# The hot gates' comparisons ahead of the weights, pieces on GpSimd, and a reordered mixer in a dense two-block kernel

## The chip, the cores and the metric

The kernel runs on one core of a Trainium2 chip. The metric is the device time of one execution in microseconds (us), lower is better. Engines are named as in the profile: PE multiplies matrices, DVE and ACT work on vectors, POOL is GpSimd, SP issues transfers. In the code they are `P`, `V`, `A`, `G` and `nc.sync`. Each engine has one queue and works through it in order; work of one engine waits for another's by semaphores.

## The reference

256 tokens of width 1024 go through two blocks, all in 32-bit floats. The first block has two layers: differential attention and a gated short convolution, each followed by a SwiGLU FFN with layer norms (LN). The second block has one layer of three parts, each added to its input behind an RMS norm:

```python
x = x + parallel_mixer(rms_norm_2(x, mix_norm_g), ...)              # mLSTM heads and stick-breaking heads
x = x + memory_cross_attention(rms_norm_2(x, xattn_norm_g), rms_norm_2(mem, mem_norm_g), ...)
x = x + peer_ffn(rms_norm_2(x, ffn_norm_g), ...)
return rms_norm_2(x, final_norm_g)
```

In the mixer, q and k of the four mLSTM heads pass a causal depthwise convolution of four taps (`qk_m = silu(causal_depthwise_conv(qk_m, conv_w, conv_b))`). The mLSTM part and the stick-breaking part are each normalised by head (`head_rms_norm`) and, side by side, multiplied by `w_out`. The memory is 256 further tokens; its keys and values are `rms_norm_2(mem) @ wkv`. PEER picks, for each token and each of 8 heads, the best 16 of 128 x 128 = 16384 experts and adds `gate * gelu(u_e . x) * v_e` over them.

## The kernel before

**Weights.** Every product of 32-bit floats is made of three matmuls (`mm3`, L328 to L331): both factors are split into a high part and a low part, `h` and `l`, and h·h, h·l and l·h are summed in PSUM. The weights come in chunks of 1 MB in the order of a plan. The class `Stream` (`W`, L195 to L262) brings them: SP issues the transfer into one of two `raw` tiles (L215); each chunk has two halves of 1024 columns, k = 0 and 1; `pre` has ACT copy a half to its high part `wh` (L231); `split` has the engine named in `W.sub[k]` subtract it from raw to give the low part `wl` (L243). `V` and `G` in `W.sub` are DVE and POOL. `W.look` says by how many halves the split runs ahead of the half that PE is about to use. The next raw transfer is issued when both halves of a chunk are split, as it reuses the tile.

**Boundaries.** Between stages the result of the last matmuls gets the residual added, is normalised and transposed to be the next stage's `xT`. The 256 tokens are two tiles t = 0 and 1 of 128. `finish_any` and, with `two=True`, `finish_two` write the order: `last_mm` (the last matmuls), `fa` (`ln_a` L412/L413 or `add_a` L458/L463, on DVE), `fb` (`ln_b` L418 to L428; `rms_b` L443 to L453, with the power (x+eps)^-0.5 on POOL, L320), `to_T` (PE transposes L370, ACT L373, DVE L378). Splits of the next weights stand between these steps, on DVE or POOL. There are three LN boundaries of the first block (`early=0`; about 134 to 150, 322 to 346 and 427 to 445 us), the one from the last FFN to the mixer (`two=True`, a LN and the RMS norm, about 612 to 650), mixer to cross attention (`early=2`, 784 to 815) and cross attention to PEER (`early=1`, 865 to 882). Matmuls on the memory (`mem_v`, `mem_k0`, `mem_k1`), which depend on nothing in the boundary, are put into it as filler; its chunks are named mv0 to mv3 here.

**The memory's copy.** The normalised memory `mT` lies in a pool that ends with the last FFN. Behind the boundary two POOL transfers (L965) copy it to a new tile, and the freed space is reused by the mixer's tiles, `vs` (L1002) among them.

**The mixer.** `mqk` (L1046 to L1064) makes q and k of one head: matmuls, a copy into a padded tile, the first tap (`tensor_scalar`, L1059, on DVE), then three more taps (L1062, on DVE); it does this for two parts, so eight taps a head. `W.sub = [G, V]` gives every k = 0 half here to POOL. A loop over `hs` then interleaves the mLSTM's outputs with the stick-breaking heads (`sb_z`, `sb_c`, `sb_v`). `ml_norm` (L1126) scales the mLSTM half of `mixed`, `sb_norm` (L1187 to L1198) the other half: a gain product on POOL (L1192) and a product by 1/rms on DVE (L1198). The products with `w_out` are interleaved with these; L362 makes a low part of a transposed operand.

**PEER's u-stage.** All 16384 experts are computed densely, in 64 chunks of two halves. The gates of the last 33 steps of this loop, the hot stage, are made from the selected slots beside the loop: for a group g of tokens `hot_make(g)` compares indices with a table on DVE (one product L1571 gives `oi`, four L1574 give `oj`, in one of two halves of the tiles OI and OJ); `hot_mm(g)` does four matmuls of 32-bit floats, eight in the trace (L1581), then multiplies `big` by the result on DVE (L1584) and copies the rest on ACT (L1585). One step e of the loop is in program order:

```python
w(k)                      # split of a later half: ACT L231, then DVE L243
while pend: pend.pop(0)() # gelu of the chunk before, on ACT
proj_stat(...)            # 24 matmuls on PE
hot_make(e - 1)           # DVE
gated()                   # the gelu's product by its gates, DVE or POOL
hot_mm(e - 2, 2 * c)      # PE, DVE L1584, ACT L1585
gated()
```

Of the kernel before, what the change touches and what calls it, by code (L numbers as in the profile page):

```python
# [197 lines left out]
class Stream:  # L198
# [36 lines left out]
    def split(self, n):  # L235
        while self.ns < min(n, 2 * len(self.plan)):
# [5 lines left out]
            for s in self.parts(self.ns):  # L242
                self.sub[k].tensor_tensor(l[:, s], self.R[i][:, k * HW:(k + 1) * HW][:, s], h.bitcast(F32)[:, s],  # L243
                                             op=OP.subtract)
# [19 lines left out]
def body(ctx, tc, I, O):  # L264
# [210 lines left out]
    def finish_two(acc, items, fa, fb, x, fa0, fb0):  # L475
# [3 lines left out]
        W.split(2 * W.i + 3)  # L479
        W.sub = [G, G]  # L480
# [24 lines left out]
    def finish_any(acc, items, fa, fb, x, fa0=(), fb0=(), two=False, early=0, first=2, warm=0):  # L505
# [14 lines left out]
        if early:  # L520
            last_mm(acc, items, 1, 1)
            W.split(2 * W.i + first + early)
# [3 lines left out]
        fa(1, 1)  # L526
        if callable(src0):
            src0 = src0()
# [431 lines left out]

    finish(acc, items, lambda t, nb: ln_a(t, nb, acc, h3), ln_rms, xT, [lambda: mem_v(0)], [lambda: mem_v(1)], True, early=0)
    f2ctx.close()
    mTo, mT = mT, new_xT()
    for k in range(2):
        G.dma_start(mT[k], mTo[k])  # L965
# [79 lines left out]
    def mqk(h, k):  # L1045
# [11 lines left out]
        for a in range(2):  # L1057
            ft = a * 4 + h
            V.tensor_scalar(y[:, a, :], pad[:, a, 0:256], cols[:, 24 + 4 * ft:25 + 4 * ft], cols[:, 56 + ft:57 + ft],  # L1059
                            op0=OP.mult, op1=OP.add)  # L1060
# [65 lines left out]
    def ml_norm(ss):  # L1126
        rs = inv_sqrt(ss, 8, "rs8")
        for t in (1, 0):
            for h in range(4):
                hs = slice(h * 128, h * 128 + 128)  # L1130
                V.tensor_scalar(mixed[:, t, hs], mixed[:, t, hs], rs[:, 4 * t + h:4 * t + h + 1], None, op0=OP.mult)
# [55 lines left out]
    def sb_norm():  # L1187
        ss = sm([128, 16], name="ss16", bufs=1)
        for t in range(2):
            sq = wp.tile([128, D], F32, name="r")[:, 0:512]  # L1190
            A.activation(sq, mixed[:, t, 512:], AF.Square)
            G.tensor_tensor(mixed[:, t, 512:], mixed[:, t, 512:], gmx[:, 512:], op=OP.mult)  # L1192
# [17 lines left out]
    W.sub = [G, V]  # L1210
# [18 lines left out]
    for hs in range(8):  # L1229
        if hs > 0:  # L1230
            sq_proj(hs // 2, hs % 2)
        if hs == 6:
            ml_norm(ss8)
# [4 lines left out]
        if i >= 0:  # L1238
            if k == 0:
                sb_z(i)  # L1240
            elif i < 2:
# [12 lines left out]
    sb_c(4)  # L1254
    to_T_half(mixed[:, 0, :], 0, mxT, 0)
    sb_c(5)
# [12 lines left out]
    W.sub = [G, V]  # L1269
    sb_norm()  # L1270
    mem_v(2)
    W.sub = [V, V]
    for t in range(2):
        to_T_half(mixed[:, t, :], t, mxT, 1)
    items = o_items(mxT, "wout", 2)
# [328 lines left out]
    for c in range(NC):  # L1604
# [4 lines left out]
        for k in range(2):  # L1609
            w(k)  # L1610
# [10 lines left out]
            e = 2 * c + k - HOT0  # L1621
# [4 lines left out]
            if 1 <= e < 34:  # L1626
                if e < 33:
                    hot_make(e - 1)
                gated()
                if e > 1:  # L1630
                    hot_mm(e - 2, 2 * c)
            gated()
        pend.append(lambda c=c, ps=ps: gelu(c, ps))
# [79 lines left out]
```

## Time and profile before

| what | us |
|---|---|
| median of three runs | 1720.41 |
| lowest and highest run | 1719.59, 1721.41 |
| the profiled execution | 1723.32 |
| its span in the trace | 1721.5 |
| mean granted PE clock in it | 0.992 |

The profiled execution is 2.9 us over the median, and 1.8 us of it lie outside the span. How to read the rows of the profile: a row of the timeline has the start, the duration, the engine, the line of the kernel, the operation, `output<-input`, partitions x elements, and `xN` where N instructions follow each other without a gap; `[3.03 <-DVE big L1584]` means that the engine was idle for 3.03 us before, until that instruction released it. A group (`L1062 DVE ... x24 | 17.9, 745 | 0.9`) has the busy time in us, the mean of one in ns, and the idle time before. A row of stretches has from:to and length, the busy time and number of instructions of PE, PEld (weight load), DVE, ACT and POOL, the granted PE clock (1.00 is full), the DMA engines' busy share and GB/s. In the list of transfers stand count, KB each and the median us to landing.

### The profile page before, as it was taken

What the parts mean: (1) busy time and instruction counts of PE and PEld (TensorE: products, weight loads), DVE (VectorE), ACT (ScalarE), POOL (GpSimd) and SP (SyncE); (2) the same over time, 40 slices, a digit from 0 to 9 for tenths busy, and PEclk for the clock granted to TensorE, in tenths of its full rate; (3) what the DMA queues carried; (4) which work ended last, traced back from release to release, by engine and by line L of the source; (5) the groups of instructions that cost most, each with busy time, mean ns of one, the idle gap of its engine ahead of it and who ended that gap; (6) DMA issues with size and microseconds to landing.
All of it is one profiled execution on the core that took longest, in us unless ns stands there. A gap on an engine that the chain in (4) does not pass through costs nothing.

```text
span 1721.5 us, 27583 instructions
## 1 busy us (share of the span) xinstructions
PE 1656.5 (96%) x11013; PEld 1505.5 (87%) x11013; DVE 1175.8 (68%) x2069; ACT 815.0 (47%) x1260; POOL 483.2 (28%) x446
## 2 busy tenths in 40 slices
PE   8899999999999998998999999999888999999997
PEld 7888999899999977887989999999887888888886
DVE  5897554667654564776558889888777666666665
ACT  5564444434444444564445545445332444444544
POOL 0542000200200022203037887788501211111111
PEclk9999999999999999999999999999999999999999
DMA  7346776455555545434355676766433566666664
GB/s 272 137 140 231 256 237 234 172 208 200 207 182 196 177 166 192 164 104 145 122 193 167 178 196 176 193 181 188 100 121 101 188 219 206 209 219 209 207 217 171
DMA packets 80416, 317.48 MB, mean 184 GB/s; under 512 B 25120, under 2 KB 41760, under 8 KB 45344
## 3 DMA queue, kind: packets, MB, share of 16 engines
q1 hardware_dynamic: 59120, 304.38, 51.7%
q0 software_dynamic: 20736, 10.56, 4.1%
q8 instruction: 86, 1.41, 0.3%
q10 hardware_dynamic: 432, 0.79, 0.1%
q14 instruction: 42, 0.34, 0.1%
HBM read 303.04 MB, written 10.55 MB: 182 GB/s over the span
## 4 chain that ended last, share of the span: by engine, by line
PE 47%; DVE 8%; issue 3%; ACT 3%; POOL 1%; DMA 1%; POOLq 0%; DVEq 0%; ACTq 0%
PE acc L331 8%; PE acc L330 7%; PE acc L329 7%; PE mm L329 7%; PE mm L331 7%; PE mm L330 7%; ACT wh L231 2%; DVE oj L1574 2%; DVE oi L1571 1%; DVE big L1584 1%; DVE wl L243 1%; DMA xTl<-mTl 1%; DVE qkm L1062 1%; POOL wl L243 0%; PE mm L1460 0%
## 5 line engine op out<-in xcount | busy, mean ns | idle before, releaser
L243 DVE TENSOR_TENSOR wl<-raw,wh 128x1024 fp32r<-128x1024 f32 (+1 forms) x511 | 631.5, 1254 | 301.6 <-ACT wh L231 300.3
L231 ACT ACTIVATE wh<-raw 128x1024 fp32r<-128x1024 f32 (+1 forms) x537 | 552.6, 1053 | 377.4 <-PE acc L331 181.7
L329 PE MATMUL mm<-xTh,wh 128*128 128x256 f32 x2328 | 660.2, 284 | 1.1 <-DVE mTl L378 1.1
L331 PE MATMUL mm<-xTh,wl 128*128 128x256 f32 x2328 | 655.8, 282 | 1.8 <-DVE wl L243 1.5
L330 PE MATMUL mm<-xTl,wh 128*128 128x256 f32 x2328 | 655.3, 281 | 0.0
L329 PEld LDWEIGHTS mm<-xTh,wh 128*128 128x128 f32 x2328 | 441.6, 190 | 3.9 <-DVE mTl L378 1.5
L331 PEld LDWEIGHTS mm<-xTh,wl 128*128 128x128 f32 x2328 | 441.3, 190 | 2.7 <-DVE wl L243 1.9
L330 PEld LDWEIGHTS mm<-xTl,wh 128*128 128x128 f32 x2328 | 441.5, 190 | 0.9
L1492 POOL DMA_INDIRECT gd<-slots,idx x128 | 259.9, 2030 | 68.9 <-issue 32.3
L329 PE MATMUL acc<-wh,xTh 128*128 128x512 f32 x632 | 249.7, 395 | 0.0
L330 PE MATMUL acc<-wl,xTh 128*128 128x512 f32 x632 | 249.2, 394 | 0.2 <-DVE wl L243 0.2
L243 POOL TENSOR_TENSOR wl<-raw,wh 128x1024 fp32r<-128x1024 f32 x26 | 64.6, 2491 | 566.8 <-ACT wh L231 565.2
L331 PE MATMUL acc<-wh,xTh 128*128 128x512 f32 x504 | 201.1, 399 | 0.0
L330 PEld LDWEIGHTS acc<-wl,xTh 128*128 128x128 f32 x632 | 119.1, 188 | 30.2 <-DVE wl L243 0.8
L329 PEld LDWEIGHTS acc<-wh,xTh 128*128 128x128 f32 x632 | 119.0, 188 | 28.7 <-issue 0.7
L1539 POOL TENSOR_TENSOR big<-big,oj 128x256 f32<-128x256 f32 x64 | 57.5, 898 | 290.3 <-DMA oj<-gd 290.3
L331 PEld LDWEIGHTS acc<-wh,xTh 128*128 128x128 f32 x504 | 94.6, 188 | 21.7
L880 DVE TENSOR_TENSOR sil<-sil,mm 128x256 f32<-128x256 f32 x44 | 18.5, 421 | 102.7 <-ACT sil L879 102.7
L879 ACT ACTIVATE sil<-mm 128x256 f32<-128x256 f32 x44 | 16.9, 385 | 148.4 <-PE mm L331 148.4
L362 DVE TENSOR_TENSOR xTh<-big,xTh 128x256 fp32r<-128x256 f32 x126 | 79.4, 630 | 0.0
L1491 POOL MEMSET spacer<- 1x1 f32 x128 | 78.9, 616 | 0.0
L330 PE MATMUL acc<-wl,hTh 128*128 128x512 f32 x176 | 69.6, 395 | 0.0
(388 smaller groups left out, 1844.2 us busy)
## 6 DMA issues: line engine op xcount, KB each, us to landing
raw<-in_ws_dram SPq DMA_DIRECT2D x131, 1024.0 KB, 5.1
raw<-in_us_dram SPq DMA_DIRECT2D x64, 1024.0 KB, 5.1
raw<-in_vs_dram SPq DMA_DIRECT2D x64, 1024.0 KB, 4.9
gd<-zt SPq DMA_DIRECT2D x32, 256.0 KB, 6.9
raw<-in_pq_dram SPq DMA_DIRECT2D x8, 1024.0 KB, 4.9
oj<-gd SPq DMA_DIRECT2D x64, 128.0 KB, 4.8
gb<-in_vec_dram POOLq DMA_DIRECT2D x12, 512.0 KB, 7.1
gd<-slots,idx POOLq DMA_INDIRECT x128, 4.0
```

The source lines that it names most:

```text
L231: self.nc.scalar.activation(h[:, s], self.R[i][:, k * HW:(k + 1) * HW][:, s], AF.Copy)
L243: self.sub[k].tensor_tensor(l[:, s], self.R[i][:, k * HW:(k + 1) * HW][:, s], h.bitcast(F32)[:, s], op=OP.subtract)
L329: P.matmul(ps, lh, rh, start=first, stop=False)
L330: P.matmul(ps, lh, rl, start=False, stop=False)
L331: P.matmul(ps, ll, rh, start=False, stop=last)
L362: V.tensor_tensor(l, src, h.bitcast(F32), op=OP.subtract)
L880: V.tensor_tensor(s, s, pg[:, 256:], op=OP.mult)
L1062: V.scalar_tensor_tensor(y[:, a, :], pad[:, a, j:j + 256], cols[:, 24 + 4 * ft + j:25 + 4 * ft + j], y[:, a, :], op0=OP.mult, op1=OP.add)
L1491: G.memset(spacer, 0.0)
L1492: d = G.indirect_dma_start(out=gd, out_offset=bass.IndirectOffsetOnAxis(ap=idx[:, h, k:k + 1], axis=0), in_=gate[:, 0, h, k:k + 1], in_off ...
L1539: G.tensor_tensor(b, b, GT.pop(c), op=OP.mult)
L1574: V.tensor_scalar(oj[:, i, :], iota, ET[:, 1, t:t + 1], ET[:, 2, t:t + 1], op0=OP.is_equal, op1=OP.mult)
```

## The change

It has eight parts. (1) A half that POOL splits is done in four pieces of 256 columns. (2) In `finish_two` the POOL split ahead of the first `fb(0)` goes; the memory's halves come behind the second power. (3) In `finish_any` with `early`, ACT's copies are made at the old place (`pre`), and the split comes behind the last `fa`, the k = 0 half on DVE and the k = 1 half on POOL. (4) The memory's copy is issued ahead of the last FFN's finish, into a tile made there. (5) The first tap of `mqk` goes from DVE to ACT (Identity with scale and bias), and all weight halves there go to DVE. (6) `ml_norm` is done by token tile: t = 1 ahead of `sb_z` at hs = 6, t = 0 behind it; `sb_c(5)` is moved ahead of the second `to_T_half`. (7) The gain product of `sb_norm` is done in two halves; `mem_v(2)` has its weights split by DVE alone with a look-ahead of one half. (8) In the u-stage `hot_make` is moved ahead of `w(k)`, and `hot_mm` behind the first `gated()`.

```diff
--- before.py
+++ after.py
@@ -239,7 +239,10 @@
                 self.mid.pop(0)()
             i, k = divmod(self.ns, 2)
             h, l = self.T[self.ns]
-            for s in self.parts(self.ns):
+            ps = self.parts(self.ns)
+            if self.sub[k] is self.nc.gpsimd:
+                ps = [slice(q, q + 256) for q in range(0, HW, 256)]
+            for s in ps:
                 self.sub[k].tensor_tensor(l[:, s], self.R[i][:, k * HW:(k + 1) * HW][:, s], h.bitcast(F32)[:, s],
                                              op=OP.subtract)
             self.ns += 1
@@ -475,8 +478,6 @@
     def finish_two(acc, items, fa, fb, x, fa0, fb0):
         last_mm(acc, items, 1, 0)
         last_mm(acc, items, 1, 1)
-        W.sub = [G, G]
-        W.split(2 * W.i + 3)
         W.sub = [G, G]
         r0 = fb(0)
         fa(1, 0)
@@ -519,11 +520,14 @@
         last_mm(acc, items, 1, 0)
         if early:
             last_mm(acc, items, 1, 1)
-            W.split(2 * W.i + first + early)
+            W.pre(2 * W.i + first + early)
         fa(1, 0)
         if not early:
             last_mm(acc, items, 1, 1)
         fa(1, 1)
+        if early:
+            W.sub = [V, G]
+            W.split(W.np - 1)
         if callable(src0):
             src0 = src0()
         W.look = 0
@@ -958,11 +962,12 @@
 
         return rest
 
+    mT2 = new_xT()
+    for k in range(2):
+        G.dma_start(mT2[k], mT[k])
     finish(acc, items, lambda t, nb: ln_a(t, nb, acc, h3), ln_rms, xT, [lambda: mem_v(0)], [lambda: mem_v(1)], True, early=0)
     f2ctx.close()
-    mTo, mT = mT, new_xT()
-    for k in range(2):
-        G.dma_start(mT[k], mTo[k])
+    mT = mT2
     mctx.close()
 
     xctx = ExitStack()
@@ -1056,8 +1061,8 @@
         y = QKM[h] = mp.tile([128, 2, 256], F32, name="qkm", bufs=4)
         for a in range(2):
             ft = a * 4 + h
-            V.tensor_scalar(y[:, a, :], pad[:, a, 0:256], cols[:, 24 + 4 * ft:25 + 4 * ft], cols[:, 56 + ft:57 + ft],
-                            op0=OP.mult, op1=OP.add)
+            A.activation(y[:, a, :], pad[:, a, 0:256], AF.Identity, bias=cols[:, 56 + ft:57 + ft],
+                         scale=cols[:, 24 + 4 * ft:25 + 4 * ft])
             for j in range(1, 4):
                 V.scalar_tensor_tensor(y[:, a, :], pad[:, a, j:j + 256], cols[:, 24 + 4 * ft + j:25 + 4 * ft + j],
                                        y[:, a, :], op0=OP.mult, op1=OP.add)
@@ -1123,12 +1128,10 @@
         V.tensor_scalar(ss, ss, 1.0 / 128, 1e-6, op0=OP.mult, op1=OP.add)
         return ss
 
-    def ml_norm(ss):
-        rs = inv_sqrt(ss, 8, "rs8")
-        for t in (1, 0):
-            for h in range(4):
-                hs = slice(h * 128, h * 128 + 128)
-                V.tensor_scalar(mixed[:, t, hs], mixed[:, t, hs], rs[:, 4 * t + h:4 * t + h + 1], None, op0=OP.mult)
+    def ml_norm(rs, t):
+        for h in range(4):
+            hs = slice(h * 128, h * 128 + 128)
+            V.tensor_scalar(mixed[:, t, hs], mixed[:, t, hs], rs[:, 4 * t + h:4 * t + h + 1], None, op0=OP.mult)
 
     SZ, SA, SQ = {}, {}, {}
 
@@ -1189,7 +1192,8 @@
         for t in range(2):
             sq = wp.tile([128, D], F32, name="r")[:, 0:512]
             A.activation(sq, mixed[:, t, 512:], AF.Square)
-            G.tensor_tensor(mixed[:, t, 512:], mixed[:, t, 512:], gmx[:, 512:], op=OP.mult)
+            for c in (slice(512, 768), slice(768, 1024)):
+                G.tensor_tensor(mixed[:, t, c], mixed[:, t, c], gmx[:, c], op=OP.mult)
             V.tensor_reduce(ss[:, 8 * t:8 * t + 8], sq.rearrange("p (a b) -> p a b", a=8), axis=AX.X, op=OP.add)
         rs = rsq(ss, 1e-6, 1.0 / 64, 16, "rs16", inv_sqrt)
         for t in range(2):
@@ -1207,7 +1211,6 @@
 
     for t in range(2):
         A.activation(vx[:, t, :, 0:128], pss[t].rearrange("p (a b) -> p a b", a=4), AF.Copy)
-    W.sub = [G, V]
     for h in range(4):
         mqk(h, 0)
         if h == 0:
@@ -1230,7 +1233,8 @@
         if hs > 0:
             sq_proj(hs // 2, hs % 2)
         if hs == 6:
-            ml_norm(ss8)
+            rs8 = inv_sqrt(ss8, 8, "rs8")
+            ml_norm(rs8, 1)
         i, k = divmod(hs - 2, 2)
         if k == 0 and i > 0:
             sb_v(2 * i - 2)
@@ -1238,6 +1242,8 @@
         if i >= 0:
             if k == 0:
                 sb_z(i)
+                if hs == 6:
+                    ml_norm(rs8, 0)
             elif i < 2:
                 sb_c(2 * i)
                 sb_c(2 * i + 1)
@@ -1252,8 +1258,8 @@
             mxT = new_xT()
     to_T_half(mixed[:, 1, :], 1, mxT, 0)
     sb_c(4)
+    sb_c(5)
     to_T_half(mixed[:, 0, :], 0, mxT, 0)
-    sb_c(5)
     acc = acc_banks()
     w_o(acc, mxT, "wout", 0, (1,))
     sb_z(3)
@@ -1266,12 +1272,12 @@
     w_o(acc, mxT, "wout", 1, (0,))
     sb_v(6)
     sb_v(7)
-    W.sub = [G, V]
     sb_norm()
+    W.look = 1
     mem_v(2)
-    W.sub = [V, V]
     for t in range(2):
         to_T_half(mixed[:, t, :], t, mxT, 1)
+    W.look = 2
     items = o_items(mxT, "wout", 2)
     xctx.close()
     h5 = hp.tile([128, 2, D], F32, name="h")
@@ -1607,6 +1613,9 @@
         if 2 * c + 2 >= NE - 32:
             assert not RU
         for k in range(2):
+            e = 2 * c + k - HOT0
+            if 1 <= e < 33:
+                hot_make(e - 1)
             w(k)
             while pend:
                 pend.pop(0)()
@@ -1618,18 +1627,13 @@
                 asplit(1)
             proj_stat(ps[:, k * 256:k * 256 + 256], w, k, xT)
             pump(CRED1)
-            e = 2 * c + k - HOT0
             if e >= 0:
                 assert not RU
             if e == 0:
                 hot_T()
-            if 1 <= e < 34:
-                if e < 33:
-                    hot_make(e - 1)
-                gated()
-                if e > 1:
-                    hot_mm(e - 2, 2 * c)
             gated()
+            if 2 <= e < 34:
+                hot_mm(e - 2, 2 * c)
         pend.append(lambda c=c, ps=ps: gelu(c, ps))
     pend.pop(0)()
     gated()
```

## The prediction

> **What bounds the kernel now.** I read the busy shares first, then what PE waited for.
>
> ```profile
> PE 1656.5 (96%) x11013; PEld 1505.5 (87%) x11013; DVE 1175.8 (68%) x2069; ACT 815.0 (47%) x1260; POOL 483.2 (28%) x446
> ```
>
> PE is busy for 96% of the span, and no edit here takes a matmul away. So an edit is worth what it removes of PE's idle time (1721.5 − 1656.5 = 65 us) and of the matmuls that run at half clock behind a gap. The waits of PE (cause: us in total, times, longest) say where that is:
>
> ```profile
> PE acc L1581 <- DVE oj L1574: 20.4, 27, 1.1
> PE mm L329 <- ACT vs L1002: 4.4, 1, 4.4
> PE mm L370 <- ACT xTh L373: 3.0, 1, 3.0
> PE mm L1204 <- DVE h L1198: 2.2, 1, 2.2
> PE mm L330 <- DVE wl L243: 1.6, 2, 0.8
> ```
>
> One place is a loop that recurs 27 times, the hot gates. The others are single stalls at stage boundaries.
>
> **A. Hot stage** (hot_make ahead of the weights' split, hot_mm last). From the timeline of PE, its hot matmuls at the first steps and at the last; then one step on DVE and ACT; then the busy times of the stretch (PE, PEld, DVE, ACT, POOL):
>
> ```profile
> 1199.99 1.05 PE L1581 MATMUL acc<-oj,oi 128*128 128x128 f32 x8
> ...
> 1211.11 1.05 PE L1581 MATMUL acc<-oj,oi 128*128 128x128 f32 x8
> ...
> 1343.53 1.17 PE L1581 MATMUL acc<-oj,oi 128*128 128x128 f32 x8 [0.62 <-DVE oj L1574]
> ```
>
> ```profile
> 1253.69 0.25 ACT L1585 ACTIVATE big<-acc 128x96 f32<-128x96 f32 x1 [3.03 <-DVE big L1584]
> 1253.84 1.05 ACT L231 ACTIVATE wh<-raw 128x1024 fp32r<-128x1024 f32 x1
> 1254.93 1.23 DVE L243 TENSOR_TENSOR wl<-raw,wh 128x1024 fp32r<-128x1024 f32 x1 [1.26 <-ACT wh L231]
> 1256.07 0.69 DVE L1571 TENSOR_TENSOR oi<-cst,ET 128x512 f32<-128x512 f32 x1
> 1256.67 1.11 DVE L1574 TENSOR_SCALAR oj<-cst,ET 128x128 f32<-128x128 f32 x4
> 1257.69 0.58 DVE L1584 TENSOR_TENSOR big<-big,acc 128x416 f32<-128x416 f32 x1
> ```
>
> ```profile
> 1300.00:1344.00 44.00, 36.61 (x292) 35.07 (x293) 33.02 (x66) 12.56 (x26) 4.50 (x4) 1.00 0.30 99
> ```
>
> The first three steps start 3.71 us apart ((1211.11 − 1199.99)/3) and show no wait: that is PE's own work. The next 28 take (1343.53 − 1211.11)/28 = 4.73. The excess is 28 × 1.02 = **28.5 us**. Its cause is a ring through three engines. PE's hot matmuls release the gate product L1584 on DVE; ACT's L1585 follows it; the next wh stands behind L1585 in ACT's queue (1.05); wl waits for wh (the 1.26 in its row) and takes 1.23; the comparisons L1571 and L1574 stand behind wl (1256.07 to 1257.69, 1.6); and PE's next hot matmuls wait for them. 0.58 + 0.25 + 1.05 + 1.23 + 1.6 = 4.7, one step. That PE waits for comparisons of the same step, though it uses those of the step before, fits that both halves of OI and OJ are one tile.
>
> After the change nothing is added or taken away, but the comparisons stand ahead of wl, so they come right behind L1584 and end 0.6 + 1.6 = 2.2 us after PE's last hot matmul. PE needs them after the step less its eight hot matmuls (1.05 at most by their row): 3.71 − 1.05 = 2.66 or later. They run beside L1585 and wh (0.25 + 1.05 = 1.3, under the 1.6 of the comparisons), so wl no longer waits: it ends at 2.2 + 1.2 = 3.4. Both are inside the step, so PE sets it. What is late next is DVE itself: its 33.02 busy us in 44 are 33.02 × 4.73/44 = 3.55 a step, 4% under 3.71. I take **−27.5**, one us left for the first and last steps. Bounds: −29.5 (one more us in the steps before 1211) and −22 (DVE at 3.9 a step in which 28 × 0.2 = 5.6 of the gain stay away).
>
> **B. The memory's move and the boundary from the FFN to the mixer.** Timeline of POOL, of DVE and of ACT there, and one stretch with its clock (the last but two of its numbers):
>
> ```profile
> 628.50 2.39 POOL L243 TENSOR_TENSOR wl<-raw,wh 128x1024 fp32r<-128x1024 f32 x1 [182.03 <-ACT wh L231]
> ...
> 636.22 2.52 POOL L243 TENSOR_TENSOR wl<-raw,wh 128x1024 fp32r<-128x1024 f32 x1
> 640.37 0.54 POOL L320 TENSOR_TENSOR rs<-ssa,nhalf 128x1 f32<-128x1 f32 x1 [1.63 <-DVE ssa L444]
> ...
> 650.19 0.54 POOL L965 DMA_DIRECT2D xTl<-mTl  x1
> ```
>
> ```profile
> 628.75 3.36 DVE L422 SCALAR_TENSOR_TENSOR r<-r,mv,gb 128x512 f32<-128x512 f32 x2
> 635.10 1.41 DVE L422 SCALAR_TENSOR_TENSOR r<-r,mv,gb 128x512 f32<-128x512 f32 x2
> ```
>
> ```profile
> 665.23 1.08 ACT L1002 ACTIVATE vs<-mm 128x512 f32<-128x512 f32 x2 [6.61 <-DMA xTl<-mTl]
> ```
>
> ```profile
> 664.80:671.50 6.70, 5.62 (x13) 4.45 (x14) 2.36 (x2) 4.86 (x6) 0.00 (x0) 0.50 0.32 100
> ```
>
> The tile vs of L1002 lies in the space that the memory leaves, so it waits 15 us for the copy (650.19 to 665.23) and PE 4.4. The clock then stands at 0.50 for 6.7 us, in which 5.62 of matmuls lose about 2.3 (an estimate, under half of 5.62). The change issues the copies ahead of the finish and into a tile of its own, so they begin some 15 us ahead of the 628.50 row (my estimate: when the last matmuls of the FFN's first part free that tile) and are done by 640 even if they take 15 us again: −6.7 in all.
>
> New costs. The copies' two transfers now stand on POOL's queue ahead of the finish and share the DMA engines with the raw chunk of the memory's weights, whose wl stands on DVE ahead of the LN. One 1 MB chunk takes 5.1 us (row below), so the delay is between 0 (the copies are through) and 5.1 (one of them is ahead of it). I take 1.9, nearer to 0, as the copies have a start of some us. The Trainium skill ("DMA: Bandwidth & Descriptors", on issuing engines that are not separate queues) has transfers of all engines interleave on the same 16 engines, which speaks against the move; the 15 us landing among weights agrees. Then mv1's two halves in eight pieces: two rows of POOL by shape price them.
>
> ```profile
> raw<-in_ws_dram SPq DMA_DIRECT2D x131, 1024.0 KB, 5.1
> ```
>
> ```profile
> L243 POOL TENSOR_TENSOR wl<-raw,wh 128x1024 fp32r<-128x1024 f32 x18 | 45.3, 2520 | 299.5 <-ACT wh L231 297.9 <-issue 1.6
> L426 POOL TENSOR_TENSOR h<-r,gb 128x512 f32<-128x512 f32 x2 | 2.5, 1290 | 0.8 <-ACT r L425 0.8
> ```
>
> 1024 columns cost 2.52, 512 cost 1.29, so 256 about 0.65 to 0.7 and eight 5.6. They start where the 636.22 half starts, behind the second power, and end near 636.2 + 5.6 = 642, or 643 with turns given to DVE. The power of 640.37 (r0's) stands behind them on POOL, DVE's r (L453) and PE's transposes behind that: 3 late; mem_v's second part waits as long for its wl. Against it, the first half of 628.50 is no longer ahead of the first power, and the two L422 beside it take 1.4 in place of 3.36: 2 earlier. 1.9 + 3 − 2 and 0.3 for the last pieces: +3.2, together **−3.5**; bounds −8 (the copies cost nothing) and +2 (a delay of 5.1, and a gap with half clock behind it).
>
> **C. The mixer's qk** (first tap to ACT, halves to DVE). DVE's groups there, one of its stretches, and POOL's group:
>
> ```profile
> L1062 DVE SCALAR_TENSOR_TENSOR qkm<-r,cols,qkm 128x256 f32<-128x256 f32 x24 | 17.9, 745 | 0.9
> L1059 DVE TENSOR_SCALAR qkm<-r,cols 128x256 f32<-128x256 f32 x8 | 5.4, 675 | 0.4 <-ACT r L1055 0.4
> ```
>
> ```profile
> 704.94 1.52 DVE L1062 SCALAR_TENSOR_TENSOR qkm<-r,cols,qkm 128x256 f32<-128x256 f32 x3
> ```
>
> ```profile
> L243 POOL TENSOR_TENSOR wl<-raw,wh 128x1024 fp32r<-128x1024 f32 x5 | 12.7, 2531 | 46.6 <-ACT wh L231 46.6
> ```
>
> An undisturbed tap is 0.51 (1.52/3); 24 of them would be 12.2, not 17.9: each POOL half holds a DVE tap for 2 us. DVE per head becomes two wl, 2.4, and six taps, 3.1: 5.5, beside PE's 48 matmuls, 5.7 at the 0.12 that A's 24 take each (2.8/24). So PE's two 0.8 waits on wl go (the row at the top); shorter ones behind the taps I put at 0.9: **−2.5**, bounds −4 and 0. An Identity of 256 columns on ACT has no row; two of 512 columns cost 1.08 (L1002), so one of 256 lies between 0.27 and 0.54, and two a head cost ACT at most 1.1 in 5.7 us. A table load has a row:
>
> ```profile
> 647.21 1.28 ACT L305 ACT_TABLE_LOAD   x1
> ```
>
> If Identity needed one each way, 2.6 us a head on ACT would keep wh late and PE's waits: that is the bound 0. I take none.
>
> **D. Order of ml_norm and sb_c.** The same instructions in other places; between −1 and +0.6, taken **−0.2**.
>
> **E. sb_norm and the boundary to cross attention.** Timeline of DVE, POOL and PE, and the clock in two stretches:
>
> ```profile
> 783.59 3.44 DVE L1198 TENSOR_TENSOR h<-h,rs 128x512 f32<-128x512 f32 x2
> 783.93 2.55 POOL L243 TENSOR_TENSOR wl<-raw,wh 128x1024 fp32r<-128x1024 f32 x1 [1.61 <-issue]
> ...
> 800.88 5.68 POOL L243 TENSOR_TENSOR wl<-raw,wh 128x1024 fp32r<-128x1024 f32 x2 [0.19 <-ACT wh L231]
> 804.92 2.19 DVE L463 TENSOR_TENSOR r<-h,gb 128x512 f32<-128x512 f32 x1
> ```
>
> ```profile
> 787.70:791.00 3.30, 3.17 (x8) 2.07 (x8) 3.22 (x5) 2.49 (x3) 0.00 (x0) 0.50 0.91 241
> ...
> 811.60:814.90 3.30, 3.30 (x17) 3.29 (x16) 2.76 (x4) 2.49 (x3) 0.00 (x0) 0.50 0.29 94
> ```
>
> Two L1198 and one L463 without a POOL half beside them would be about 1.4 and 0.7 (L463's row in F); they take 2.0 and 1.5 more. Without the half of 783.93 PE's 2.2 us wait goes, and with it the half clock behind it (half of 3.3, 1.6): 3.8. I give all of it back: with a look-ahead of one half wout's next wl come later by about 2 us, and what follows waits for a raw chunk and its wh in any case. The halves of sb_norm's gain on POOL cost nothing, as nothing else stands there.
>
> At the boundary POOL's 5.68 us come in pieces behind the power. L463's 1.5 and some 1 of the L453 before it go from the chain to the first matmuls: −2.5. PE's wait of 3.0 gets shorter by as much, and with a chance of one half the clock stays up behind it, which is worth 1.6: −0.8. Together **−3.3**, bounds −6 and 0 (the pieces hold the next power as long).
>
> The Trainium skill ("TensorE: Matmul & The Clock Gate", "Why this matters for your kernels") has the clock fall behind PE gaps of more than about 3 us. By that rule the shortened gap costs no clock at all, and the sum would be 0.8 lower. The trace here differs: it fell behind a wait of 2.2.
>
> **F. The boundary to PEER.** L463 there stands beside a POOL half too:
>
> ```profile
> 872.47 0.69 DVE L463 TENSOR_TENSOR r<-h,gb 128x512 f32<-128x512 f32 x1
> ...
> 874.22 1.75 DVE L463 TENSOR_TENSOR r<-h,gb 128x512 f32<-128x512 f32 x1
> ```
>
> 1.75 − 0.69 = 1.06, of which I take **−0.9**; bounds −1.5 and +0.5.
>
> **G. Pieces at the three LN boundaries.** POOL has one half at each; in four pieces it costs 0.1 (4 × 0.65 against 2.52) to 0.5 more, and a matmul that waits for the last piece as much: three times 0.1 to 0.65, so 0 to +2, taken **+0.7**.
>
> **Sum.** −27.5 − 3.5 − 2.5 − 0.2 − 3.3 − 0.9 + 0.7 = −37.2. The profiled execution took 1723.3, 2.9 more than the median of 1720.4, from which I subtract: **1683**.
>
> **Rivals.**
> 1. DVE bounds the hot step. For it: 4% margin. Against: the comparisons come early enough. At 3.85 a step the gain is 28 × 0.88 = 24.6 and less at the ends, 22 to 24: 1687 to 1689. It lies inside the range; chance 0.2.
> 2. The hot stage doesn't move: wl turns out to be what PE waits for, as the comparisons now stand ahead of it. Then only −9.7 is left: 1711. Against: wl has two halves of look-ahead, 7.4 us. Chance 0.05.
> 3. Slower: the comparisons wait for PE to release their buffers (two of them), wl stands behind them, and PE uses up its look-ahead. The step is then a ring of PE 3.71, comparisons 1.6 and wl 1.23, 6.5 us: 28 × 1.8 = +50, less 9.7: 1761. It decides once DVE lags by more than two halves, 7.4 us. Chance 0.03.
> 4. The boundaries give the gain back: the eight pieces ahead of the mixer's powers and the copies in the weights' way leave B at +2 and E at 0: 1683 + 5.5 + 3.3 = 1692. Chance 0.15.
>
> **How the numbers follow.** My forecast, with PE bounding the hot step and the boundaries as summed, has 0.57. A good case of all bounds is unlikely together; A, B and E at two thirds of their good ends give 1683 − 1.4 − 3 − 1.8 = 1677, and with C 1676; I go to 1673. Above, rivals 1 and 4 together reach 1689 + 8.8 = 1698, so the range is 1673 to 1698, without rivals 2 and 3. A measurement tells about 0.2% (3.4 us) from no change. Within it are the cases in which rivals 2 and 4 come together (1711 + 8.8 = 1720): 0.03. Slower are rival 3 and 0.01 for these two with a half clock more: 0.04. Faster: 0.93.
>
> **What would show it.** A: L1581 3.7 apart with no wait on L1574; wait on wl instead means rival 2 or 3. B: L1002 without a DMA wait and no 0.50 at 665; in exchange a longer gap ahead of the transposes at 645. C: L1062 at 0.51 throughout and no table load. E: L1198 at 1.4 for its two; no 0.50 at 788. The prediction is wrong if the hot steps stay over 4 us, or a boundary shows a gap that was not there.

## The result and the profile after

| | us |
|---|---|
| before, median of 4 runs | 1720.0 (1717.75 to 1721.41) |
| after, median of 4 runs | 1692.8 (1691.32 to 1695.26) |
| ratio | 0.9844, 95% interval 0.9827 to 0.9862 |
| profiled execution, before and after | 1723.32, 1691.32 |

The change takes 27 us off, 10 less than the prediction's sum of 37. The two profiled executions lie 32.0 apart, as that of before is 3.3 over its median and that of after 1.5 under its own; ledgers made from the two traces are too large by about 5 us in all.

The page and the waits of PE, after the change:

```profile
PE 1645.5 (97%) x11013; PEld 1500.7 (89%) x11013; DVE 1166.5 (69%) x2069; ACT 819.2 (48%) x1268; POOL 469.7 (28%) x494
```

```profile
PE mm L332 <- ACT wh L231: 9.2, 3, 6.6
PE mm L334 <- DVE wl L246: 3.7, 4, 1.8
PE mm L333 <- POOL wl L246: 3.3, 2, 3.2
PE mm L334 <- POOL wl L246: 2.5, 1, 2.5
PE mm L373 <- DVE r L451: 3.0, 2, 1.7
```

The 20.4 us on the comparisons are gone, and so are the waits on vs and on h; the one of 3.0 at the transposes is down to 1.7 (L373). In their place stand waits on the two parts of the weights, wh and wl: two new ones on wh, 9.2 - 6.6 = 2.6 (the 6.6 is the first load of the program, 6.5 before), and 3.2 and 2.5 on POOL's wl.

The start of the same matmul in the two traces shows where the time went. PE does the same work in the same order up to the mixer's later part (760 us), so the difference between the two columns changes only where something was won or lost:

| PE at | before | after | difference |
|---|---|---|---|
| transposes of the LN boundary at 341 | 341.78 | 340.52 | -1.3 |
| transposes of the LN boundary at 441 | 441.54 | 442.44 | +0.9 |
| a gate matmul of the last FFN | 455.75 | 461.24 | +5.5 |
| first gate matmul of the mixer (L979) | 645.64 | 653.89 | +8.3 |
| decays' transposes, behind vs | 673.45 | 674.35 | +0.9 |
| first mLSTM scores, behind qk | 720.29 | 717.92 | -2.4 |
| last sb_v | 778.45 | 776.52 | -1.9 |
| first transposes of the boundary to cross attention | 806.44 | 802.46 | -4.0 |
| its last transposes | 811.41 | 805.47 | -5.9 |
| transposes of the boundary to PEER | 877.59 | 871.67 | -5.9 |
| first PEER scores (L1460) | 890.60 | 888.78 | -1.8 |
| first hot matmul (L1581) | 1199.99 | 1198.65 | -1.3 |
| hot matmuls, 32nd step | 1344.05 | 1314.00 | -30.1 |

Two thirds of the way the change is nearly even (-1.3 at 1200): the LN boundaries and what follows them cost 6.8 (2.2 by the transposes at 441, and 4.6 right behind them), the boundary to PEER 4.6 (-5.9 to -1.3), and these eat what the mixer, the memory's move and sb_norm gain. Everything that is left is the hot stage.

**The hot stage after.** PE's hot matmuls at the first, the fourth and the 32nd step, then one step of DVE, then the busy times of a stretch:

```profile
1198.65 1.05 PE L1587 MATMUL acc<-oj,oi 128*128 128x128 f32 x8
...
1209.77 1.05 PE L1587 MATMUL acc<-oj,oi 128*128 128x128 f32 x8
...
1313.56 1.05 PE L1587 MATMUL acc<-oj,oi 128*128 128x128 f32 x8
```

```profile
1251.63 0.59 DVE L1590 TENSOR_TENSOR big<-big,acc 128x424 f32<-128x424 f32 x1 [0.28 <-PE acc L1587]
1252.14 0.68 DVE L1577 TENSOR_TENSOR oi<-cst,ET 128x512 f32<-128x512 f32 x1
1252.75 1.11 DVE L1580 TENSOR_SCALAR oj<-cst,ET 128x128 f32<-128x128 f32 x4
1253.77 1.22 DVE L246 TENSOR_TENSOR wl<-raw,wh 128x1024 fp32r<-128x1024 f32 x1
1255.41 0.60 DVE L1590 TENSOR_TENSOR big<-big,acc 128x432 f32<-128x432 f32 x1 [0.42 <-PE acc L1587]
```

```profile
1300.00:1314.00 14.00, 14.00 (x124) 14.00 (x122) 12.01 (x23) 5.67 (x12) 2.14 (x3) 1.00 0.40 126
```

The 28 steps behind the fourth take (1313.56 - 1209.77)/28 = 3.71 each, PE is busy without a gap, and the direction of the wait has turned: DVE waits 0.3 to 0.4 us a step for PE (L1590 on L1587). In the step shown, wl follows the comparisons with no wait for wh.

**The LN boundaries after.** POOL before, POOL after, then ACT before and after, then PE and the clock after:

```profile
440.17 4.74 POOL L243 TENSOR_TENSOR wl<-raw,wh 128x1024 fp32r<-128x1024 f32 x2 [2.43 <-ACT wh L231]
```

```profile
441.06 7.56 POOL L246 TENSOR_TENSOR wl<-raw,wh 128x256 fp32r<-128x256 f32 x8 [2.43 <-ACT wh L231]
```

```profile
450.53 2.01 ACT L231 ACTIVATE wh<-raw 128x1024 fp32r<-128x1024 f32 x2 [0.77 <-DMA raw<-in_ws_dram]
```

```profile
455.94 2.00 ACT L231 ACTIVATE wh<-raw 128x1024 fp32r<-128x1024 f32 x2 [5.19 <-DMA raw<-in_ws_dram]
```

```profile
457.04 0.39 PE L332 MATMUL mm<-xTh,wh 128*128 128x256 f32 x1 [1.93 <-ACT wh L231]
```

```profile
458.30:461.70 3.40, 3.40 (x16) 3.40 (x17) 2.40 (x4) 1.95 (x3) 0.00 (x0) 0.50 0.85 266
```

Two halves of POOL take 7.56 in pieces and 4.74 whole. Most of the eight pieces take 0.74 each; the last two, which meet DVE's own splits (L246), take 1.72 each. DVE's two splits take 3.27 beside the pieces and 3.28 beside the whole halves, so DVE gained nothing from the cutting here. The raw tile is free only when the last piece is done, at 448.6 in place of 444.9, so the next chunk is asked for 3.7 later (0.9 of it because the whole boundary comes later). ACT's wh comes 5.4 later, as the transfer itself takes longer too: another chunk is asked for 0.4 behind it, where it was 2.2 before, and loads of gains run beside both. Their share was not tried by itself. PE waits 1.93, and the clock falls to 0.50 behind that gap.

**The boundary to PEER after.** POOL before and after, then ACT, PE and DVE after:

```profile
872.65 2.76 POOL L243 TENSOR_TENSOR wl<-raw,wh 128x1024 fp32r<-128x1024 f32 x1 [2.27 <-ACT wh L231]
876.38 0.54 POOL L320 TENSOR_TENSOR rs<-ssa,nhalf 128x1 f32<-128x1 f32 x1 [0.96 <-DVE ssa L444]
876.88 0.68 POOL L1363 DMA_DIRECT2D hs<-h  x1
```

```profile
870.00 0.55 POOL L323 TENSOR_TENSOR rs<-ssa,nhalf 128x1 f32<-128x1 f32 x1 [4.95 <-DVE ssa L447]
870.52 2.97 POOL L246 TENSOR_TENSOR wl<-raw,wh 128x256 fp32r<-128x256 f32 x4
873.44 0.61 POOL L1369 DMA_DIRECT2D hs<-h  x1
```

```profile
882.56 0.60 ACT L1458 ACTIVATE big<-mm 128x512 f32<-128x512 f32 x1 [5.37 <-DMA hs<-h]
```

```profile
884.55 0.39 PE L334 MATMUL mm<-xTh,wl 128*128 128x256 f32 x1 [2.52 <-POOL wl L246]
```

```profile
884.13 6.25 DVE L246 TENSOR_TENSOR wl<-raw,wh 128x1024 fp32r<-128x1024 f32 x1 [8.51 <-ACT wh L231]
```

The power comes 6.4 earlier than before (5.9 of it had been won ahead of this boundary), but the copy of h into hs, which in the old order followed the power at once, now stands behind four pieces of weights. `big` lies in the space of h; its first write on ACT (L1458) waits 5.4 for that copy, the next wh stands behind it in ACT's queue, POOL's pieces behind wh, and PE waits 2.5, with a half clock after it.

### The profile page after: what moved, and what is told of

Its sections match the earlier page's. It is cut to its first block, busy times and chain, and to the rows that moved or that the text cites. A ratio compares the mean times of both kernels' runs of the same rounds, so it can differ in the third digit from the quotient of the medians.

```text
span 1689.5 us, 27640 instructions
## 1 busy us (share of the span) xinstructions
PE 1645.5 (97%) x11013; PEld 1500.7 (89%) x11013; DVE 1166.5 (69%) x2069; ACT 819.2 (48%) x1268; POOL 469.7 (28%) x494
## 4 chain that ended last, share of the span: by engine, by line
PE 82%; DVE 6%; issue 3%; POOL 3%; DMA 2%; ACT 2%; POOLq 0%; ACTq 0%; DVEq 0%
PE mm L332 16%; PE mm L334 16%; PE mm L333 16%; PE acc L333 10%; PE acc L332 9%; PE acc L334 9%; DVE wl L246 3%; PE acc L1587 2%; DMA raw<-in_ws_dram 2%; POOL wl L246 1%; ACT wh L231 1%; POOL rs L323 1%; DMA hs<-h 1%; POOL h L429 0%; PE mm L1342 0%
## 5 line engine op out<-in xcount | busy, mean ns | idle before, releaser
L246 DVE TENSOR_TENSOR wl<-raw,wh 128x1024 fp32r<-128x1024 f32 (+1 forms) x519 | 643.8, 1260 | 263.9 <-ACT wh L231 262.5
L1498 POOL DMA_INDIRECT gd<-slots,idx x128 | 253.6, 1981 | 67.9 <-issue 32.0
L246 POOL TENSOR_TENSOR wl<-raw,wh 128x256 fp32r<-128x256 f32 x72 | 55.9, 809 | 325.0 <-ACT wh L231 324.9
```

Of the source, the lines that this page charges most:

```text
L1498: d = G.indirect_dma_start(out=gd, out_offset=bass.IndirectOffsetOnAxis(ap=idx[:, h, k:k + 1], axis=0), in_=gate[:, 0, h, k:k + 1], in_off ...
```

## The experiments

Times are medians; before was at 1720.3 to 1721.2 beside them.

**Which part does it.** `hot_only` is the kernel before with this alone:

```diff
+            e = 2 * c + k - HOT0
+            if 1 <= e < 33:
+                hot_make(e - 1)
             w(k)
...
-            if 1 <= e < 34:
-                if e < 33:
-                    hot_make(e - 1)
-                gated()
-                if e > 1:
-                    hot_mm(e - 2, 2 * c)
             gated()
+            if 2 <= e < 34:
+                hot_mm(e - 2, 2 * c)
```

> The kernel before with the hot stage's new order alone (part 8). Theory: the hot stage is worth 28 to 30 us and all other parts together about nothing, because the LN boundaries (+6) and the boundary to PEER (+4) give back what the mixer's parts and the memory's move gain. Then this kernel is at 1690 to 1693, as the changed kernel, its hot steps 3.7 apart, and its trace shows the old waits at L1002, L1198 and L1062. Rival: the rest of the change is worth the 9.7 of the prediction, and the hot stage only some 18: then this is at about 1702.

1692.4, ratio 0.9833 (0.9820 to 0.9847), with hot steps 3.71 apart, and PE's old wait on vs (L1002) still there with 4.3.

`no_hot` is the changed kernel with these lines the other way round:

> The changed kernel with the hot stage in the old order. Theory: 1718 to 1722, no difference from before that can be told; hot steps 4.7 apart again. Rival (the rest is worth 9.7): about 1710.

1722.7, ratio 1.0014 (1.0005 to 1.0023), 0.7 above the theory's range: the seven other parts together cost 2.4 us here, and 0.4 when the changed kernel is set against `hot_only`. The theory holds in the main, the rival falls: the new order of the hot stage (the comparisons moved ahead, hot_mm moved back; the two were not tried apart) makes the whole result, and the rest gives back as much as it gains.

**What closes the ring of the hot stage.** `oi_tiles`, in the kernel before:

```diff
-    OI = bx.tile([128, 2, 4, 128], F32, name="oi", bufs=1)
-    OJ = bx.tile([128, 2, 4, 128], F32, name="oj", bufs=1)
...
-        oi, oj = OI[:, g % 2], OJ[:, g % 2]
+        oi = bx.tile([128, 4, 128], F32, name="oi", bufs=2)
+        oj = bx.tile([128, 4, 128], F32, name="oj", bufs=2)
...
```

Two later tiles in the same space are cut in two to match.

> The kernel before, with the old order, but each half of the comparisons' results (oi, oj) as a tile of its own. Theory of the prediction: PE waits for comparisons of the step after its own because both halves are one tile, and the ring goes through PE; without that link the hot steps fall to about 3.7 and the time to about 1692. Rival: the ring closes on DVE and ACT alone (gate product L1584, ACT's copy L1585 behind it, wh behind that, wl, comparisons, and the next gate product behind them in DVE's queue: 0.58 + 0.25 + 1.05 + 1.23 + 1.6 = 4.7); then the steps stay at 4.7, the wait of PE only gets another name, and the time stays at 1720.

1721.5 in one run, and PE's wait is the same to the last digit:

```profile
PE acc L1580 <- DVE oj L1573: 20.4, 27, 1.1
```

The prediction's link by one shared tile is wrong. PE waits for the very comparisons that it uses: in the trace of before, the 32nd group of `oj` runs from 1343.05 to 1344.16 and PE's 32nd hot matmuls start at 1343.53. They are late because DVE and ACT alone go round in 4.7 us and fall behind. `copy_dve`, in the kernel before, old order:

```diff
-        A.activation(b[:, J:, :], pv[:, J:, :], AF.Copy)
+        V.tensor_copy(b[:, J:, :], pv[:, J:, :])
```

> The kernel before, with the copy behind the gate product (L1585) on DVE in place of ACT; order and comparisons as before. If ACT's queue is a link of the ring (wh stands behind L1585), wh no longer waits, wl and the comparisons come 1.3 us earlier, and the step is PE's 3.7 or DVE's own work, 3.55 + 0.25 = 3.8: 1692 to 1697. Rival (what costs is that the comparisons stand behind wl on DVE, whatever ACT does): 4.7 stays, 1720.

1688.6 in one run, with the steps at 3.71. Its first and 32nd hot matmuls are (1309.90 - 1195.00)/31 = 3.71 apart, and the stretch between shows who else is near the bound:

```profile
1195.00 1.05 PE L1581 MATMUL acc<-oj,oi 128*128 128x128 f32 x8
...
1309.90 1.05 PE L1581 MATMUL acc<-oj,oi 128*128 128x128 f32 x8
```

```profile
1195.00:1310.00 115.00, 115.00 (x995) 115.00 (x994) 112.62 (x255) 41.54 (x64) 37.99 (x37) 1.00 0.47 147
```

With the comparisons still behind wl, it is enough that wh no longer stands behind a copy that waits for DVE. DVE is then busy for 112.62 of 115, 98%: PE still bounds, by a hair. The cause is the ring through ACT's queue, and the reordering is one of two ways to cut it. (Its trace is 4.3 shorter than that of `hot_only`: 2.2 of this lie in the first 55 us, which differ from run to run, and 1.9 at a half clock at 812 that it missed.)

**Pieces.** `whole` undoes part 1 in the changed kernel:

```diff
-            ps = self.parts(self.ns)
-            if self.sub[k] is self.nc.gpsimd:
-                ps = [slice(q, q + 256) for q in range(0, HW, 256)]
-            for s in ps:
+            for s in self.parts(self.ns):
```

> The changed kernel with POOL's halves in one piece again (part 1 undone). Theory: the eight pieces behind each LN boundary take 7.6 us where two whole halves took 4.75, so a raw tile comes free 2.8 later, the next chunk lands later and ACT's wh, then PE, wait (2.1 at 455 with a half clock behind it, 0.9 twice at 358). Without pieces these waits go: 5 to 7 us less, 1686 to 1688. The wait of 2.7 at 882 stays, as it hangs on the copy of h. Rival: the waits on wh come from elsewhere (the gains' loads, the memory's copy, chance): 1692, waits still there.

1689.6, 3.2 less, half of what was expected. By the starts of PE the LN boundaries gain 7.6, somewhat more than the theory says; but at the three boundaries with powers, where pieces had kept a POOL half off a power or off DVE, all of it is given back by 875, and the clock stands at 0.50 for 16.8 us in all, where the changed kernel's profile had 6.8 (3.4 at 806 and 3.4 at 885):

```profile
636.40:643.10 6.70, 5.13 (x12) 4.07 (x13) 5.93 (x6) 1.44 (x4) 4.85 (x3) 0.50 0.21 45
800.20:807.00 6.80, 5.51 (x25) 5.30 (x26) 5.68 (x7) 3.08 (x4) 1.43 (x2) 0.50 0.64 232
871.90:875.20 3.30, 3.30 (x16) 3.30 (x17) 2.40 (x3) 1.28 (x2) 0.00 (x0) 0.50 0.87 258
```

Behind that 2.6 come back, as PE's wait at 884 falls from 2.5 to 1.7 and has no half clock behind it. So pieces cost where a raw tile is waited for and pay where a short chain passes through POOL and DVE, though a part of those half clocks may be chance (last section).

**The copy of h.** `hs_early`, in the changed kernel:

```diff
-    G.dma_start(hs, h6)
...
+    def rms_hs(t):
+        r = rms_b(h6[:, t, :], ("ss", t), gf)
+        if t == 1:
+            G.dma_start(hs, h6)
+        return r
```

> The changed kernel with the copy of h (hs) issued on POOL right behind the second power of the boundary to PEER, ahead of the weight's pieces. Theory: the pieces that now stand ahead of that transfer (2.97 us) hold up its landing, ACT's first write into the space of h waits 5.4 for it, the next wh stands behind, and PE loses 2.7 and a half clock at 882: with the copy 3 us earlier 3 to 4.5 us go, 1688 to 1690, and the clock stays at 1.00 there. Rival: the wl itself is late because the pieces are slow: the wait stays within 1 us, 1692.

1691.7, 1.1 less, and nearer to the rival's time. The waits of 5.4 and 2.5 are gone, which is the theory, and with them and their half clock 4.9 us in PE's starts; but 3.9 had been lost just before, at 870 to 877. POOL and DVE there:

```profile
869.69 0.55 POOL L323 TENSOR_TENSOR rs<-ssa,nhalf 128x1 f32<-128x1 f32 x1 [4.94 <-DVE ssa L447]
870.20 0.61 POOL L1371 DMA_DIRECT2D hs<-h  x1
870.83 2.76 POOL L246 TENSOR_TENSOR wl<-raw,wh 128x256 fp32r<-128x256 f32 x4
```

```profile
870.27 3.60 DVE L451 TENSOR_SCALAR r<-r,rs 128x512 f32<-128x512 f32 x1 [0.66 <-POOL rs L323]
```

L451 took 0.94 in the changed kernel and 3.60 here: issued just behind the start of POOL's transfer, it ended 0.3 after the last of the four pieces. It stands in the chain to the transposes.

`cut_hs` therefore issues the copy ahead of the power and cuts halves only in the boundaries with powers (`early`, `two`), not in the LN boundaries or later:

```diff
+            if self.cut and self.sub[k] is self.nc.gpsimd:
...
+        if t == 1:
+            G.dma_start(hs, h6)
+        return rms_b(h6[:, t, :], ("ss", t), gf)
```

> The changed kernel with whole POOL halves at the three LN boundaries and elsewhere, pieces only in the boundaries with powers behind them (FFN to mixer, mixer to cross attention, to PEER), and the copy of h issued on POOL ahead of the second power there. Theory: the LN boundaries lose their 7 us as with whole halves, the pieces keep their 2 us each at 640, 800 and 871, and the copy of h doesn't hold PE at 882, without a longer L451: 1692.8 - 7 - 4 = 1681 to 1683. Rival: the boundaries trade waits for half clocks whatever is done, as whole halves (-3.2) and the earlier copy (-1.1) did: 1688 to 1690.

1679.8, ratio to before 0.9764 (0.9751 to 0.9777); against the changed kernel 13.0 less, 1.2 below the range expected. POOL and DVE at PEER's boundary, and ACT's wh behind the LN boundary:

```profile
861.65 0.61 POOL L1373 DMA_DIRECT2D hs<-h  x1 [4.10 <-DVE h L462]
862.51 0.56 POOL L324 TENSOR_TENSOR rs<-ssa,nhalf 128x1 f32<-128x1 f32 x1 [0.25 <-DVE ssa L448]
863.05 2.98 POOL L247 TENSOR_TENSOR wl<-raw,wh 128x256 fp32r<-128x256 f32 x4
```

```profile
863.11 0.95 DVE L452 TENSOR_SCALAR r<-r,rs 128x512 f32<-128x512 f32 x1 [0.69 <-POOL rs L324]
```

```profile
454.16 2.01 ACT L232 ACTIVATE wh<-raw 128x1024 fp32r<-128x1024 f32 x2 [0.61 <-DMA raw<-in_ws_dram]
```

The copy stands in time in which POOL was idle, DVE's product is at 0.95, and the wait on the raw chunk is 0.6 again. The two misses of the prediction are thereby undone, each by its own cause: by PE's starts the LN boundaries get 7.8 back, and from 878 to 897, where the changed kernel lost 4.7, `cut_hs` loses nothing.

**The boundary to the mixer**, on top of `cut_hs`. `cut_hs_gv`:

```diff
+        W.sub = [G, V]
         W.split(2 * W.i + 2)
+        W.sub = [G, G]
         src0 = r0()
```

> As the one before, and of the memory's two halves behind the second power of the boundary to the mixer the k = 1 half goes to DVE. Theory: r0's power stands behind four pieces in place of eight (642 to 648.6 in the changed kernel, while DVE was idle for 4.0 us), so the transposes come 2 to 3 us earlier and PE's wait of 3.2 on POOL's wl stays: 2 to 3 less than the one before, 1679 to 1681. Rival: DVE holds the POOL pieces up as much as POOL held DVE, and PE waits for the same wl: no difference.

1680.1, no difference: the rival. r0's power did come 1.8 earlier (640.07 for 641.84 in `cut_hs`), but PE was not there: it still waited 3.5 for the first four pieces, and the transposes stand behind those matmuls.

`cut_hs_move` puts the memory's copy back behind the boundary (part 4):

```diff
-    mT2 = new_xT()
-    for k in range(2):
-        G.dma_start(mT2[k], mT[k])
     finish(acc, items, ...)
...
+    mTo, mT = mT, new_xT()
+    for k in range(2):
+        G.dma_start(mT[k], mTo[k])
```

> The kernel cut_hs with the memory's copy behind the boundary again (part 4 undone). Theory: the old wait of L1002 and its half clock come back (+7), and the first memory weights land 2 to 3 us earlier, as no copy competes with them (7 to 8 us from issue to ACT's wh with the copy, 4.9 without): net +4 to +5, 1684 to 1685. Rival (the copy costs the boundary as much as it frees): no difference.

1684.6, 4.8 more, as expected. Its wait on vs is back:

```profile
PE mm L333 <- ACT vs L1009: 5.0, 1, 5.0
```

`cut_hs_two` splits once more ahead of the first power (undoes part 2):

```diff
+        W.sub = [G, G]
+        W.split(2 * W.i + 3)
         W.sub = [G, G]
         r0 = fb(0)
```

> The kernel cut_hs with a POOL split ahead of the first power of the boundary to the mixer again (part 2 undone; in pieces). Theory: the first power comes 2 to 3 us later, as the pieces stand ahead of it, but only four pieces stand ahead of r0's power and PE gets its wl earlier, so the wait of 3.8 on POOL's wl at 633 shrinks: between -1 and +1. Prediction's reading (the half ahead of the first power costs 2 net of nothing): +2.

1677.4, 2.5 less than `cut_hs`, more than either reading gave it. POOL:

```profile
627.00 2.83 POOL L247 TENSOR_TENSOR wl<-raw,wh 128x256 fp32r<-128x256 f32 x4 [15.66 <-ACT wh L232]
629.79 1.01 POOL L324 TENSOR_TENSOR rs<-rs1a,nhalf 128x1 f32<-128x1 f32 x1
```

POOL had been idle for 15.7 us; the pieces end 0.4 after the power's input is ready (629.37), so the half ahead of the power costs next to nothing there. r0's power then stands behind four pieces and begins 0.6 after its input, in `cut_hs` 3.4, and PE's wait on POOL's wl falls from 3.5 to 1.8.

`cut_hs_sp` leaves the copy to SP, behind the raw chunk of sv0:

```diff
-    for k in range(2):
-        G.dma_start(mT2[k], mT[k])
+    mT1 = mT
+    W.after.setdefault(front.index(("sv", 0)), []).append(
+        lambda: [nc.sync.dma_start(mT2[k].bitcast(F32), mT1[k].bitcast(F32)) for k in range(2)])
```

> The kernel cut_hs with the memory's copy issued by SP behind the raw chunk of the mixer's first weights (sv0), so that it runs 8 us later than now, clear of the memory's own weights. Theory: mv0's raw lands 5 us after its issue in place of 7 to 8, the boundary comes 2 to 3 us earlier, and the copy is still done before L1002 asks for its space: 1677 to 1678. Rival: the boundary is bound by POOL's pieces and powers, or the copy now delays sv0 as it delayed mv0: no difference.

1677.9, 1.9 less, as expected. ACT waited 5.73 in `cut_hs` for the transfer of the memory's first weights; now the transfer is there in time, and ACT waits 3.71 for PE to release a tile:

```profile
620.63 2.01 ACT L232 ACTIVATE wh<-raw 128x1024 fp32r<-128x1024 f32 x2 [3.71 <-PE acc L335]
```

`best` has both edits:

> The kernel cut_hs with both: the POOL split ahead of the first power again (as cut_hs_two) and the memory's copy issued by SP behind the raw chunk of sv0 (as cut_hs_sp). If the two gains are of different causes (two: four pieces in place of eight between mem_v and r0's power; sp: the raw of the memory's first weights), they add for the most part: 1679.8 - 2.5 - 1.9, so 1675 to 1676, with no half clock in the boundary. Rival: both shorten the same wait on POOL's wl and the same half clock; then this is no better than either, 1677 to 1678.

1677.2 (ratio to before 0.9744, 0.9729 to 0.9759): the rival. Both shorten the same wait of PE on POOL's wl (3.5 in `cut_hs`, 1.4 to 1.8 in these three). POOL's rows in `best` show why they don't add:

```profile
628.30 3.74 POOL L247 TENSOR_TENSOR wl<-raw,wh 128x256 fp32r<-128x256 f32 x4 [181.82 <-ACT wh L232]
632.00 0.56 POOL L324 TENSOR_TENSOR rs<-rs1a,nhalf 128x1 f32<-128x1 f32 x1
```

The half ahead of the power was nearly free in `cut_hs_two` only because the copy delayed the weights and with them the LN. In `best` the weights are in time again, the pieces begin 0.3 ahead of the power's input (L329 is done at 628.64), and they hold the power for 3.4. Three versions at 1677 to 1678 beat the changed kernel by 15 us, 0.9%, and none of them the others by more than the runs differ.

## Why the prediction was right or wrong

The forecast was 1683 with a range of 1673 to 1698; 1692.8 lies inside, 9.8 over. A carried it as forecast. Parts 1 to 7, which were to give 9.7, gave nothing, and by the prediction's own second sign (a boundary with a gap that was not there) its account of the boundaries was wrong in two places: PE has new gaps of 1.9 at 457, 3.2 at 644 and 2.5 at 884. The one at 644 was priced, in B; the other two, in G and F, were not.

- **A, the hot stage: right in size, wrong in one link.** -27.5 predicted, 27.9 by `hot_only`. DVE had more margin than the 4% it was given (busy for 93.8 of the 103.8 us of the 28 steps, 3.35 a step where 3.55 was reckoned), so neither rival 1, 2 nor 3 came. The ring was described through PE and a shared tile; `oi_tiles` shows that it closes on DVE and ACT alone, and `copy_dve` that ACT's queue is a link of it.
- **B, the move and the boundary to the mixer: -3.5 predicted, -4.6 in the traces** (+2.8 from 456 to 654, -7.4 at vs). Its terms came about as they were summed. The memory's first weights come 2.1 later (ACT waits 5.55 for their transfer, 3.47 before; 1.9 booked). The first power begins 0.1 after its input (L328 done at 636.63, power at 636.72), where it began 2.0 after (L325 done at 628.83, power at 630.87; 2 booked). r0's power begins 3.4 after its own input, which is ready at 645.22 (3 booked). The move alone is worth 4.8 by `cut_hs_move`, with the delay inside it. What the step did not see is that the delay changes what part 2 is worth: while the LN waits for the weights POOL is idle, and a half ahead of the power then costs 0.4 instead of 2 and spares r0's power four pieces, so that part 2, in the kernel with the move, loses the 2.5 that `cut_hs_two` gets back. Without the delay (`best`) the half holds the power for 3.4, and nothing is won.
- **C, qk: -2.5 predicted, -3.3 in the traces.** DVE's taps there are down to one price, and there is no table load at the new line:

```profile
L1067 DVE SCALAR_TENSOR_TENSOR qkm<-r,cols,qkm 128x256 f32<-128x256 f32 x24 | 11.3, 484 | 2.9 <-ACT qkm L1064 2.4
```

```profile
L1064 ACT ACTIVATE qkm<-r,cols 128x256 f32<-128x256 f32 x8 | 4.4, 594 | 0.7 <-ACT r L1060 0.4
```

  The Identity costs ACT 0.55 (4.4/8), just over the 0.54 that was its bound, and ACT found room: DVE's taps wait 2.4 us for it in all, and part 5 still gains.
- **D: -0.2 predicted, +0.4** (-2.4 to -1.9 in the table), within its bounds.
- **E, sb_norm and its boundary: -3.3 predicted, -4.0** (-1.9 to -5.9). L1202 (before L1198) takes 1.29 for its two, and the wait of 3.0 fell to 1.7. The split of it was wrong: 2.1 come at sb_norm (-1.9 to -4.0), which was booked at nothing because the raw chunk would take it back, and 1.9 at the boundary, booked at 3.3. The rule on gaps of about 3 us from the Trainium skill ("TensorE: Matmul & The Clock Gate", "Why this matters for your kernels") didn't hold here: behind the shortened gap the clock fell all the same in this execution (window 806.40 below).

```profile
781.04 1.29 DVE L1202 TENSOR_TENSOR h<-h,rs 128x512 f32<-128x512 f32 x2
```

```profile
806.40:809.80 3.40, 3.40 (x18) 3.40 (x17) 3.26 (x4) 2.02 (x3) 0.76 (x2) 0.50 0.69 196
```

- **F, the boundary to PEER: -0.9 predicted, +4.6 in the traces.** L466 fell from 1.75 to 0.69 as the step says. What failed is that only arithmetic was counted as standing behind the moved split: a transfer stood there as well, and the space that it frees.
- **G, the pieces at the LN boundaries: +0.7 predicted, +6.8 in the traces.** The step priced one half there, POOL's longer time and the matmul that waits for the last piece. There are two more behind the second power, and what they hold is the raw tile: `whole` and `cut_hs` got 7.6 and 7.8 back with it. G misses by 6.1 and F by 5.5: together the 12 us between the -9.7 that parts 1 to 7 were given and the +2.4 of `no_hot`. Rival 4 had boundaries that give the gain back, and its 1692 is almost the measured time, but that is luck: it had B at +2 and E at 0, which came at -4.6 and -4.0, and neither the raw tile nor the copy of h was in it.

## What to carry to other kernels

Where an engine waits once a step, add up the ring of queue orders that closes there; here either of the two links that were cut was enough, and the cheaper one was a copy on the wrong engine. When work is moved behind a short operation, list what stood directly behind that operation, the transfers first, and whose memory each of them frees. Cutting work into pieces for another engine's sake made the whole of it longer (7.56 for 4.74), and the buffer that it reads stayed taken for as long. A gain measured beside one delay can vanish with the delay, so two edits that shorten the same stretch are best tried together.

## What the runs showed of the hardware that had not been expected

Pieces that follow each other on POOL don't always let a waiting DVE instruction in between. L451 took 3.60 beside one transfer and four pieces of 2.76 in all, and a split of 1.22 took 6.25 beside eight pieces of 5.53 in all. But in the changed kernel L451 took 0.94 beside the same four pieces, and at the LN boundary two DVE splits took 3.27 and held two of the pieces for 1.72 each in place of 0.74. Which side gets its way was not settled.

A gap of the same length can cost a half clock in one execution and none in another. In `cut_hs` and in `best` PE waits as long at the boundary to cross attention (both lists have this row):

```profile
PE mm L374 <- DVE r L452: 3.1, 2, 1.8
```

The stretch behind it, in `cut_hs` and then in `best`:

```profile
799.00:802.40 3.40, 3.15 (x26) 2.91 (x27) 3.01 (x5) 2.76 (x4) 2.36 (x4) 1.00 0.27 41
```

```profile
798.40:801.70 3.30, 3.24 (x15) 3.24 (x16) 3.11 (x4) 2.39 (x4) 1.13 (x2) 0.50 0.50 137
```

The Trainium skill ("TensorE: Matmul & The Clock Gate", Part 1) says that the window which watches PE runs freely and isn't tied to the program; the two rows agree with that. By PE's starts the half clock costs `best` 1.5 us there, so the half clocks of a single profile are not to be booked as a gain or a loss.
